# Two weight blocks' low parts moved from VectorE to GpSimd, and a diagonal matrix from VectorE to ScalarE, at the seam between a feed-forward layer and a convolution

## The chip, the cores and the metric

The kernel runs on one core of a Trainium2 chip. The metric is the device time of one execution in microseconds (us). Before the change three runs took 934.97, 930.46 and 936.47 us; their median is 934.97 us. Besides these there is one profiled execution, which took 930.08 us; its trace has a span of 928.3 us.

The engines are named as in the profile: PE is the matrix engine (TensorE) and PEld its weight load, DVE is VectorE, ACT is ScalarE, POOL is GpSimd, SP is SyncE, which issues most of the DMAs.

## The reference

A trunk of two layers over 256 tokens of width 1024, all in fp32. Each layer is a feed-forward block at half weight, a mixer, and a second feed-forward block; the mixer of the first layer is a convolution module, that of the second an attention. The part that matters here is the end of the first feed-forward block of layer 0 and the convolution behind it:

```
h = h + 0.5 * swiglu_ffn(rmsnorm(h, g1), w1, w3, w2)      # (silu(x w1) * (x w3)) w2
m = rmsnorm(h, mix_norm)
u = m @ w_pw1                      # 1024 -> 2048
a, b = split(u);  u = a * sigmoid(b)
u = causal depthwise convolution of width 31 over time
u = silu(rmsnorm(u, g_norm))
h = h + u @ w_pw2                  # 1024 -> 1024, the convolution's last layer
```

## The kernel before

**Split operands.** Most matmuls are done in three passes. A weight block (128 x 2048) is loaded by SP into a `raw` buffer, ACT rounds it to a high part (`hi`, L161), and DVE takes the difference as a low part (`lo`, L162), each in two pieces of 128 x 1024 (`PIECES` is 2). `mm3` (L271 to L275) then multiplies low by high, high by high and high by low. There are four `raw` buffers and four `hi`/`lo` pairs, used in turn: the load of a block waits until the block four places earlier has been read for the last time. Blocks are listed in one fixed order (`blocks`), and SP issues their loads in that order, so that a load which waits holds up those behind it. A block marked "whole" has no high and low part; its `raw` buffer is read by the matmuls.

The list for the convolution begins with two blocks of the last layer (`cw2[0]` and `cw2[1]`, `conv_block[-1]` and `conv_block[-2]`), which are split and lie ready until the convolution's end. Behind them come the eight blocks of the first layer, whole (`cw1[0]` to `cw1[7]`), and the two remaining blocks of the last layer.

**The end of the feed-forward block.** The output of the down projection (`o`, four PSUM tiles: token block 0 or 1 by column half 0 or 1) is partly computed by a scheme that trades matmuls for additions (`fast`); it ends in `fold` (L551 to L559), which adds the partial sums in PSUM (`p`) to the residual `h`: DVE forms L553, L554, L556 and L558, and POOL adds L552, L555, L557 and L559 to `h`. Then `finish` runs the last matmuls tile by tile and adds each tile to `h` on DVE (L566).

**The norm in front of the convolution** (`Plain`). When a column half of `h` is done, ACT squares and sums it (L298). After both halves of token block 0 ACT also loads the table for the sigmoid and runs it once (L422). POOL turns the sum into 1/rms in three small steps (L303, L304, L306; the last is a power). `diagonal` (L427) multiplies the identity by it on DVE, and PE multiplies `h` by this diagonal matrix `dR` (L433), which transposes and normalizes at once; ACT and DVE evict the result by gain (L442, L444). The second half of the matmuls of the last output tile is ordered behind the turn of token block 0, and the turn of token block 1 behind the first product of the convolution.

**The convolution.** PE computes `gate` and `u` (L717) for eight channel blocks; ACT and DVE form `V` (L724, L725). The 31 taps are shared out: DVE has most channel blocks (L759, L761), POOL adds the products that ACT makes for three of them (L775, L779, L780, L781), PE does the rest as matmuls (L790). Then come the second norm (L808 to L840) and the last layer (L901 and `mm3`).

**What sets the order.** The framework simulates the program and orders each engine's instructions by it; a function marked `@urgent` goes ahead of other ready work; `behind` keeps the splits behind the last six urgent instructions of an engine; `order` adds a fixed order between two instructions. Each engine runs its own queue strictly in order.

Of the kernel before, what the change touches and what calls it, by code (L numbers as in the profile page):

```python
# [11 lines left out]
F32 = mybir.dt.float32  # L12
# [3 lines left out]
AF = mybir.ActivationFunctionType  # L16
ALU = mybir.AluOpType
# [24 lines left out]
PIECES = 2  # L42
# [38 lines left out]
def trunk(ctx: ExitStack, tc: tile.TileContext, x, xt, pos, invf, gains, gfin, wdw,  # L81
          f1w13, f1w2, f2w13, f2w2, cw1, cw2, wa, wuq, wukv, wo, out):
    nc = tc.nc
# [12 lines left out]
    def uid(s):  # L96
        n_uid[0] += 1
        return f"{s}_{n_uid[0]}"
# [10 lines left out]
    conv_block = {}  # L109
# [20 lines left out]
    loaded = []  # L130
# [4 lines left out]
    def order(ins, first):  # L135
        tc.add_manual_dep(ins.ins, first.name, mybir.DependencyInfo(
            mybir.DependencyClass.NoSync, mybir.DependencyReason.DATA), reason="order")

    def behind(ins):

        for first in ahead_of.get(ins.ins.engine, [])[-BEHIND:]:
            order(ins, first)

    def load(src, pieces=1):
        if isinstance(src, tuple) and src[0] == "fast":
            return load_fast(src[1])
        if isinstance(src, tuple):
            raw = rawp.tile([P, HB], F32, tag="raw", name=uid("raw"))
            nc.sync.dma_start(raw, src[1])
            return raw  # L150
        n = src.shape[-1]
        raw = rawp.tile([P, HB], F32, tag="raw", name=uid("raw"))
        hi = wp.tile([P, HB], F32R, tag="hi", name=uid("hi"))
        lo = wp.tile([P, HB], F32R, tag="lo", name=uid("lo"))
        if len(loaded) < 7:
            fetch(raw[:, :n], src)
        else:
            nc.sync.dma_start(raw[:, :n], src)
        for i in range(pieces):
            c = slice(i * n // pieces, (i + 1) * n // pieces)  # L160
            behind(nc.scalar.copy(hi[:, c], raw[:, c]))  # L161
            behind(nc.vector.tensor_sub(lo[:, c], raw[:, c], hi[:, c].bitcast(F32)))  # L162
        return hi, lo

    def load_fast(src):

        raw = rawp.tile([P, HB], F32, tag="raw", name=uid("raw"))
        sums = rawp.tile([P, HB], F32, tag="raw", name=uid("sums"))
        nc.sync.dma_start(raw, src)
        v = raw.rearrange("p (b n) -> p b n", n=512)  # L170
        t = sums.rearrange("p (b n) -> p b n", n=512)
        behind(nc.gpsimd.tensor_tensor(t[:, 0:2, :], v[:, 0:4:3, :], v[:, 1:2, :].to_broadcast([P, 2, 512]), op=ALU.add))  # L172
        behind(nc.vector.tensor_add(t[:, 2, :], t[:, 0, :], v[:, 3, :]))
        behind(nc.vector.tensor_add(t[:, 3, :], t[:, 2, :], v[:, 2, :]))
        out = []
        for x, cols in ((raw, ((0, 512), (1024, 2048))), (sums, ((0, 1024), (1024, 2048)))):
            hi = wp.tile([P, HB], F32R, tag="hi", name=uid("hi"))
            lo = wp.tile([P, HB], F32R, tag="lo", name=uid("lo"))
            for c0, c1 in cols:
                behind(nc.scalar.copy(hi[:, c0:c1], x[:, c0:c1]))  # L180
                behind(nc.vector.tensor_sub(lo[:, c0:c1], x[:, c0:c1], hi[:, c0:c1].bitcast(F32)))  # L181
            out.append((hi, lo))
        return out
# [24 lines left out]
    def load_to(last):  # L208
        while len(loaded) < last:
            loaded.append(load(blocks[len(loaded)], PIECES))  # L210
# [23 lines left out]
    def fetch(to, src):  # L234

        dma = nc.sync.dma_start(to, src)
        if first_dma:
            order(dma, first_dma[-1].ins)
        first_dma.append(dma)

    fetch(xk[:, :1], xt[:, :1])
    for k in range(KT):
        c = slice(k % 4 * 512, k % 4 * 512 + 512)
# [5 lines left out]
    ident = const.tile([P, P], F32, name="ident")  # L249
    make_identity(nc, ident)  # L250
    neghalf = const.tile([P, 1], F32, name="neghalf")
# [36 lines left out]
    def rstd(src, n, name, scale_in=1.0):  # L288

        ss = small.tile([P, 2], F32, tag="ss", name=uid("ss"))  # L290
        for i in range(2):
            squares(ss, src, n, i, scale_in)
        return power(ss, n, name)

    def squares(ss, src, n, i, scale_in=1.0):
# [2 lines left out]
        nc.scalar.activation(junk[:, :nh], src[:, i * nh:(i + 1) * nh], AF.Square, scale=scale_in,  # L298
                             accum_out=ss[:, i:i + 1])

    def power(ss, n, name):
        ms = small.tile([P, 2], F32, tag="ms", name=uid("ms"))
        nc.gpsimd.tensor_tensor(ms[:, 0:1], ss[:, 0:1], ss[:, 1:2], op=ALU.add)  # L303
        nc.gpsimd.tensor_scalar(ms[:, 1:2], ms[:, 0:1], 1.0 / n, EPS, op0=ALU.mult, op1=ALU.add)  # L304
        r = small.tile([P, 1], F32, tag="r", name=uid(name))
        nc.gpsimd.tensor_tensor(r, ms[:, 1:2], neghalf, op=ALU.pow)  # L306
        return r

    def transposed(src, q, n, after=(), turned=None):
# [25 lines left out]
    class Norm:  # L335
# [26 lines left out]
        def early(self, i):  # L362

            if i == 1:
                self.part(0, 0)
            elif i == 2:
                self.part(0, 1)
                self.rms(0)
            elif i == 3:
                self.part(1, 0)  # L370
# [35 lines left out]
    class Plain:  # L406
# [17 lines left out]
        @urgent  # L424
        def diagonal(self, tb):
            r = power(self.ss[tb], D, "R")
            nc.vector.tensor_scalar(self.dg[tb], ident, r, None, op0=ALU.mult)  # L427

        @urgent
        def turn(self, tb, q, after=()):  # L430
# [15 lines left out]
        def early(self, i):  # L446
            self.half(i // 2, i % 2)
            if i % 2 == 1:
                self.diagonal(i // 2)
            if i == 2:  # L450

                for q in range(2):
                    self.turn(0, q)
# [822 lines left out]
def build(shapes):  # L1276
    import concourse.bacc as _bacc

    nc = _bacc.Bacc("TRN2", target_bir_lowering=False, num_devices=1, dynamic_dma_scratch_size=1024)
    args = [nc.dram_tensor(f"in_{n}", s, mybir.dt.from_np(np.dtype(d)), kind="ExternalInput").ap()  # L1280
            for n, s, d in shapes]
    out = nc.dram_tensor("out", (S, D), F32, kind="ExternalOutput").ap()
    with tile.TileContext(nc, schedule_with_timeline_sim=True) as tc:
        trunk(tc, *args, out)
    return nc
# [9 lines left out]
```

## Time and profile before

| | |
|---|---|
| Three runs | 934.97, 930.46, 936.47 us (median 934.97) |
| Profiled execution | 930.08 us, of which 928.3 us span |
| PE busy | 913.5 us, 98% of the span |
| DVE busy | 687.6 us, 74% |
| ACT busy | 536.4 us, 58% |
| POOL busy | 213.4 us, 23% |
| Bytes moved | 191.58 MB, 206 GB/s in the mean |

A row of the timeline is: start in us, duration in us (of the whole merged group), engine, line, operation, output <- input, shape, count, and in brackets the idle time of the engine before it and what ended it. [...] A row of the stages gives the stage, its length, the busy time of PE, PEld, DVE, ACT and POOL with the number of instructions, the granted PE clock, the share of the DMA engines and the GB/s.

### The profile page before, as it was taken

The numbers are of one execution on the slowest core, as the hardware profiler recorded it, in microseconds if no ns is written. First come the engines' busy times: TensorE is split into PE (matmuls) and PEld (weight loads), VectorE is DVE, ScalarE is ACT, GpSimd is POOL, SyncE is SP. The second block draws the span as 40 slices with busy tenths as digits, with TensorE's granted clock in tenths as the row PEclk, the third lists the DMA queues.
The fourth block names the chain that finished last, engine by engine and source line by source line (L and its number), as shares of the span: only waits on it lengthen the run. The fifth ranks groups of instructions, "written<-read, shape, count | busy, mean of one in ns | idle before, by whom it ended". The sixth has DMA issues, their size and how long they took to land.

```text
span 928.3 us, 12409 instructions
## 1 busy us (share of the span) xinstructions
PE 913.5 (98%) x4337; PEld 761.0 (82%) x4337; DVE 687.6 (74%) x1047; ACT 536.4 (58%) x928; POOL 213.4 (23%) x325
## 2 busy tenths in 40 slices
PE   9999999899999999999999999999999999999997
PEld 7888888798977888888888888888898778888886
DVE  5777787889974667778876667878666476667975
ACT  6964465558865445455575445655667374544643
POOL 1110222349931001222210003223200010003223
PEclk9999999999999999999999999999999999999999
DMA  9986555823323866565857765657451557774651
GB/s 340 348 291 231 203 170 216 317 90 139 137 91 127 299 243 237 184 196 198 308 198 237 246 233 184 193 206 262 181 182 46 182 204 236 254 246 150 226 181 46
DMA packets 60399, 191.58 MB, mean 206 GB/s; under 512 B 11184, under 2 KB 33328, under 8 KB 40752
## 3 DMA queue, kind: packets, MB, share of 16 engines
q1 hardware_dynamic: 59760, 190.09, 58.7%
q8 instruction: 34, 0.56, 0.2%
q10 hardware_dynamic: 576, 0.69, 0.2%
q14 instruction: 29, 0.24, 0.1%
HBM read 178.17 MB, written 12.58 MB: 205 GB/s over the span
## 4 chain that ended last, share of the span: by engine, by line
PE 89%; DVE 5%; ACT 3%; DMA 1%; issue 1%; SPq 0%; POOLq 0%; ACTq 0%; POOL 0%; DVEq 0%
PE u L275 17%; PE u L271 17%; PE u L274 17%; PE o L271 6%; PE o L274 6%; PE o L275 6%; DVE lo L162 3%; PE u L717 3%; PE gate L717 3%; PE p L275 2%; PE p L271 2%; PE p L274 2%; PE o L901 2%; PE y L790 2%; ACT hi L161 1%
## 5 line engine op out<-in xcount | busy, mean ns | idle before, releaser
L162 DVE TENSOR_TENSOR lo<-raw,hi 128x1024 fp32r<-128x1024 f32 (+1 forms) x250 | 304.9, 1255 | 76.9 <-ACT hi L161 76.8
L161 ACT CAST hi<-raw 128x1024 fp32r<-128x1024 f32 (+1 forms) x250 | 248.0, 1046 | 153.3 <-PE u L275 111.1
L275 PE MATMUL u<-hi,Xl 128*128 128x512 f32 x688 | 267.8, 390 | 0.7 <-DVE Xl L330 0.7
L271 PE MATMUL u<-lo,Xh 128*128 128x512 f32 x688 | 268.1, 390 | 0.1
L274 PE MATMUL u<-hi,Xh 128*128 128x512 f32 x688 | 267.7, 389 | 0.0
L275 PEld LDWEIGHTS u<-hi,Xl 128*128 128x128 f32 x688 | 129.2, 188 | 28.5 <-DVE Xl L330 1.6
L271 PEld LDWEIGHTS u<-lo,Xh 128*128 128x128 f32 x688 | 129.2, 188 | 26.8 <-DVE lo L162 0.5
L274 PEld LDWEIGHTS u<-hi,Xh 128*128 128x128 f32 x688 | 129.2, 188 | 26.8
L271 PE MATMUL o<-lo,Gh 128*128 128x512 f32 (+1 forms) x236 | 91.0, 386 | 0.0
L275 PE MATMUL o<-hi,Gl 128*128 128x512 f32 (+1 forms) x236 | 91.0, 385 | 0.0
L274 PE MATMUL o<-hi,Gh 128*128 128x512 f32 (+1 forms) x236 | 91.0, 385 | 0.0
L172 POOL TENSOR_TENSOR sums<-raw 128x1024 f32<-128x1024 f32 x20 | 53.1, 2653 | 161.2 <-DMA raw<-in_f2w 52.6
L611 POOL TENSOR_TENSOR sx<-gb 128x128 f32<-128x128 f32 x20 | 10.4, 521 | 311.9 <-DMA gb<-gd 311.9
L181 DVE TENSOR_TENSOR lo<-sums,hi 128x1024 fp32r<-128x1024 f32 x40 | 56.1, 1433 | 0.0
L603 ACT CAST Gh<-gb 128x512 fp32r<-128x512 f32 (+2 forms) x48 | 25.6, 539 | 49.8 <-DMA gb<-gd 49.6
L761 DVE SCALAR_TENSOR_TENSOR acc<-V,dw,acc 128x256 f32<-128x256 f32 (+1 forms) x160 | 54.0, 417 | 0.1
L180 ACT CAST hi<-sums 128x1024 fp32r<-128x1024 f32 x40 | 40.7, 1052 | 22.5 <-PE u L275 15.3
L604 DVE TENSOR_TENSOR Gl<-gb,Gh 128x512 fp32r<-128x512 f32 (+2 forms) x48 | 33.1, 704 | 26.4 <-ACT Gh L603 26.4
L275 PEld LDWEIGHTS o<-hi,Gl 128*128 128x128 f32 x236 | 44.3, 188 | 9.0
L274 PEld LDWEIGHTS o<-hi,Gh 128*128 128x128 f32 x236 | 44.3, 188 | 9.0
L271 PEld LDWEIGHTS o<-lo,Gh 128*128 128x128 f32 x236 | 44.3, 188 | 8.7
L180 ACT CAST hi<-raw 128x512 fp32r<-128x512 f32 (+1 forms) x40 | 31.4, 834 | 34.7 <-PE o L275 27.8
(246 smaller groups left out, 1336.6 us busy)
## 6 DMA issues: line engine op xcount, KB each, us to landing
raw<-in_f2w SPq DMA_DIRECT2D x66, 1024.0 KB, 4.8
raw<-in_f1w SPq DMA_DIRECT2D x64, 1024.0 KB, 5.3
raw<-in_cw SPq DMA_DIRECT2D x12, 1024.0 KB, 6.0
gd<-gt SPq DMA_DIRECT2D x160, 64.0 KB, 2.5
gb<-gd SPq DMA_DIRECT2D x40, 256.0 KB, 3.0
raw<-in_wo SPq DMA_DIRECT2D x4, 1024.0 KB, 4.9
raw<-in_wuq SPq DMA_DIRECT2D x3, 1024.0 KB, 4.7
raw<-in_f1w SPq DMA_DIRECT2D x8, 256.0 KB, 6.2
```

Source lines behind the costliest of these rows:

```text
L161: behind(nc.scalar.copy(hi[:, c], raw[:, c]))
L162: behind(nc.vector.tensor_sub(lo[:, c], raw[:, c], hi[:, c].bitcast(F32)))
L172: behind(nc.gpsimd.tensor_tensor(t[:, 0:2, :], v[:, 0:4:3, :], v[:, 1:2, :].to_broadcast([P, 2, 512]), op=ALU.add))
L180: behind(nc.scalar.copy(hi[:, c0:c1], x[:, c0:c1]))
L181: behind(nc.vector.tensor_sub(lo[:, c0:c1], x[:, c0:c1], hi[:, c0:c1].bitcast(F32)))
L271: mm = nc.tensor.matmul(o, ah, bl, start=start, stop=False)
L274: nc.tensor.matmul(o, ah, bh, start=False, stop=False)
L275: return nc.tensor.matmul(o, al, bh, start=False, stop=stop)
L603: nc.scalar.copy(dh, x)
L604: nc.vector.tensor_sub(dl, x, dh.bitcast(F32))
L717: mm = nc.tensor.matmul(u[:, t], w[:, c], X.x[:, k, t], start=(k == 0), stop=(k == KT - 1))
L761: nc.vector.scalar_tensor_tensor(out if j == j1 - 1 else y, v, w, y, op0=ALU.mult, op1=ALU.add)
```

## The change

Two things change, both at this seam.

The low parts of the two split blocks `cw2[0]` and `cw2[1]` are no longer taken by DVE when the blocks are loaded. Their operands are kept in a list (`low_later`), and `lows` takes them by POOL, two pieces (one block) behind the power of each of the norm's two token blocks. The diagonal matrix is made by ACT (a copy of the identity, scaled by the 1/rms of each row) and no longer by DVE.

```diff
+    low_later = []
+
     def load(src, pieces=1):
...
+        later = len(loaded) in (conv_block[-1], conv_block[-2])
...
             behind(nc.scalar.copy(hi[:, c], raw[:, c]))
-            behind(nc.vector.tensor_sub(lo[:, c], raw[:, c], hi[:, c].bitcast(F32)))
+            if later:
+                low_later.append((lo[:, c], raw[:, c], hi[:, c].bitcast(F32)))
+            else:
+                behind(nc.vector.tensor_sub(lo[:, c], raw[:, c], hi[:, c].bitcast(F32)))
...
+    raised = []
+
     def power(ss, n, name):
...
-        nc.gpsimd.tensor_tensor(r, ms[:, 1:2], neghalf, op=ALU.pow)
+        raised.append(nc.gpsimd.tensor_tensor(r, ms[:, 1:2], neghalf, op=ALU.pow))
...
         def diagonal(self, tb):
             r = power(self.ss[tb], D, "R")
-            nc.vector.tensor_scalar(self.dg[tb], ident, r, None, op0=ALU.mult)
+            nc.scalar.activation(self.dg[tb], ident, AF.Copy, scale=r)
+
+        def lows(self, n):
+
+            for _ in range(n):
+                order(nc.gpsimd.tensor_tensor(*low_later.pop(0), op=ALU.subtract), raised[-1].ins)
...
             if i % 2 == 1:
                 self.diagonal(i // 2)
+                self.lows(PIECES)
```

On DVE, from the last splits of the feed-forward block to the turn of token block 0, the queue before was as follows (`lo_1538` and `lo_1546` are the low parts of the two blocks, `h_79` and `h_80` the two token blocks of the residual, `o_1193` to `o_1195` the first three output tiles):

```order
L162 TENSOR_TENSOR lo_1495<-raw_1493,hi_1494 128x1024 x2
L162 TENSOR_TENSOR lo_1538<-raw_1536,hi_1537 128x1024
L553 TENSOR_TENSOR fold_1525<-p_1206,fold_1522 128x512
L162 TENSOR_TENSOR lo_1538<-raw_1536,hi_1537 128x1024
L554 TENSOR_TENSOR fold_1523<-p_1207,fold_1525 128x512
L556 TENSOR_TENSOR fold_1526<-p_1208,fold_1525 128x512
L162 TENSOR_TENSOR lo_1546<-raw_1544,hi_1545 128x1024 x2
L558 TENSOR_TENSOR fold_1524<-p_1208,fold_1523 128x512
L566 TENSOR_TENSOR h_79<-o_1193,h_79 128x512
L566 TENSOR_TENSOR h_79<-o_1194,h_79 128x512
L566 TENSOR_TENSOR h_80<-o_1195,h_80 128x512
L427 TENSOR_SCALAR dR_1568<-ident,R_1592 128x128
```

In the changed kernel (whose line numbers are up to 14 higher; L567 to L572 are the fold, L580 the addition to `h`) the same stretch is:

```order
L168 TENSOR_TENSOR lo_1495<-raw_1493,hi_1494 128x1024 x2
L567 TENSOR_TENSOR fold_1525<-p_1206,fold_1522 128x512
L568 TENSOR_TENSOR fold_1523<-p_1207,fold_1525 128x512
L570 TENSOR_TENSOR fold_1526<-p_1208,fold_1525 128x512
L572 TENSOR_TENSOR fold_1524<-p_1208,fold_1523 128x512
L580 TENSOR_TENSOR h_79<-o_1193,h_79 128x512
L580 TENSOR_TENSOR h_79<-o_1194,h_79 128x512
L580 TENSOR_TENSOR h_80<-o_1195,h_80 128x512
L457 TENSOR_SCALAR Xp_1561<-tp_1608,G 128x128
```

The four subtractions between the fold's steps are gone, and so is the diagonal matrix.

On POOL, behind the fold's last addition, stood the norm of the two token blocks, the clearing of the padding of `V`, and then the taps:

```order
L559 TENSOR_TENSOR h_80<-h_80,fold_1524 128x512
L303 TENSOR_TENSOR ms_1589<-ss_1566 128x1
L304 TENSOR_SCALAR ms_1589<-ms_1589 128x1
L306 TENSOR_TENSOR R_1592<-ms_1589,neghalf 128x1
L705 MEMSET V 128x8x30
L303 TENSOR_TENSOR ms_1643<-ss_1567 128x1
L304 TENSOR_SCALAR ms_1643<-ms_1643 128x1
L306 TENSOR_TENSOR R_1646<-ms_1643,neghalf 128x1
L780 TENSOR_TENSOR Y<-Y,prod_2078 128x128
```

In the changed kernel the two blocks' subtractions (L440) stand behind each power (L314):

```order
L573 TENSOR_TENSOR h_80<-h_80,fold_1524 128x512
L311 TENSOR_TENSOR ms_1585<-ss_1562 128x1
L312 TENSOR_SCALAR ms_1585<-ms_1585 128x1
L314 TENSOR_TENSOR R_1588<-ms_1585,neghalf 128x1
L440 TENSOR_TENSOR lo_1538<-raw_1536,hi_1537 128x1024 x2
L719 MEMSET V 128x8x30
L311 TENSOR_TENSOR ms_1641<-ss_1563 128x1
L312 TENSOR_SCALAR ms_1641<-ms_1641 128x1
L314 TENSOR_TENSOR R_1644<-ms_1641,neghalf 128x1
L440 TENSOR_TENSOR lo_1544<-raw_1542,hi_1543 128x1024 x2
L794 TENSOR_TENSOR Y<-Y,prod_2078 128x128
```

The second token block's norm and the first tap now each have two subtractions of 128 x 1024 in front of them.

On ACT, in the changed kernel, each diagonal matrix (L435) stands behind the squares of its token block (L304), the first one also behind the table load and the sigmoid (L430):

```order
L304 ACTIVATE junk_1566,ss_1562<-h_79 128x512
L304 ACTIVATE junk_1581,ss_1562<-h_79 128x512
L430 ACT_TABLE_LOAD
L430 ACTIVATE sigm<-ss_1562 128x1
L435 ACTIVATE dR_1564<-ident,R_1588 128x128
L304 ACTIVATE junk_1606,ss_1563<-h_80 128x512
```

Before, the third square followed the sigmoid directly; no further table load was added.

## The prediction

> **What bounds the kernel now.** I read the page first: the busy times, and the chain that ended last.
>
> ```profile
> span 928.3 us, 12409 instructions
> PE 913.5 (98%) x4337; PEld 761.0 (82%) x4337; DVE 687.6 (74%) x1047; ACT 536.4 (58%) x928; POOL 213.4 (23%) x325
> PE 89%; DVE 5%; ACT 3%; DMA 1%; issue 1%; SPq 0%; POOLq 0%; ACTq 0%; POOL 0%; DVEq 0%
> ```
>
> PE is the bound, and the chain leaves it for little. So an edit on DVE, ACT and POOL gains only where PE waits, and at most that wait. Next come the stages around the seam.
>
> ```profile
> 168.00:182.50 14.50, 14.48 (x64) 11.64 (x63) 13.15 (x12) 6.65 (x8) 6.44 (x4) 1.00 0.85 310
> 182.50:188.80 6.30, 3.45 (x24) 3.22 (x25) 2.10 (x6) 4.55 (x12) 1.38 (x4) 1.00 0.37 155
> 188.80:246.00 57.20, 57.20 (x336) 52.27 (x335) 54.49 (x163) 44.63 (x124) 46.53 (x95) 1.00 0.37 130
> ```
>
> PE is idle in the middle stage alone (3.45 of 6.30 us busy); ahead of it DVE is nearly full (13.15 of 14.50), behind it PE never rests for 57 us. The timeline of PE shows the wait as one hole:
>
> ```profile
> 178.01 0.39 PE L275 MATMUL o<-hi,Gl 128*128 128x512 f32 x1
> 182.09 0.39 PE L275 MATMUL o<-hi,Gl 128*128 128x512 f32 x1
> 185.35 2.02 PE L433 MATMUL tp<-dR,h 128*128 128x128 f32 x16 [2.87 <-ACT sigm L422]
> 193.74 1.95 PE L433 MATMUL tp<-dR,h 128*128 128x128 f32 x16
> ```
>
> The row names the sigmoid, but what the matmul reads is `dR`. Where that was late, the other engines' timelines tell, DVE's first:
>
> ```profile
> 165.39 2.35 DVE L162 TENSOR_TENSOR lo<-raw,hi 128x1024 fp32r<-128x1024 f32 x2
> 169.33 4.60 DVE L162 TENSOR_TENSOR lo<-raw,hi 128x1024 fp32r<-128x1024 f32 x3 [1.59 <-ACT hi L161]
> 176.78 4.18 DVE L162 TENSOR_TENSOR lo<-raw,hi 128x1024 fp32r<-128x1024 f32 x2
> 180.88 0.68 DVE L558 TENSOR_TENSOR fold<-p,fold 128x512 f32<-128x512 f32 x1
> 181.48 1.87 DVE L566 TENSOR_TENSOR h<-o,h 128x512 f32<-128x512 f32 x3
> 184.96 0.29 DVE L427 TENSOR_SCALAR dR<-ident,R 128x128 f32<-128x128 f32 x1 [1.61 <-POOL R L306]
> ```
>
> The three additions to `h` (L566) begin at 181.48, right behind the last fold. The second of them reads the output tile whose last matmul began at 178.01, so it stood about 3 us behind four pieces of L162 that nobody needs before the convolution's end. ACT and POOL then follow without a pause:
>
> ```profile
> 183.00 0.63 ACT L298 ACTIVATE junk<-h 128x512 f32<-128x512 f32 x1
> 183.54 0.19 ACT L298 ACTIVATION_READ_ACCUMULATOR junk<-h 128x1 f32 x1
> 183.74 1.28 ACT L422 ACT_TABLE_LOAD   x1
> 185.04 0.20 ACT L422 ACTIVATE sigm<-ss 128x1 f32<-128x1 f32 x1
> 184.36 0.57 POOL L306 TENSOR_TENSOR R<-ms,neghalf 128x1 f32<-128x1 f32 x1
> ```
>
> The squares end at 183.73, the power at 184.93, `dR` at 185.25, and PE starts at 185.35. The releaser is DVE's queue.
>
> **The part on DVE: what goes, and what is late next.** L162 loses its last four pieces here. They cost more than their own work:
>
> ```profile
> 170.80 2.04 POOL L552 TENSOR_TENSOR h<-h,fold 128x512 f32<-128x512 f32 x1 [12.93 <-ACT fold L551]
> 176.34 1.30 POOL L555 TENSOR_TENSOR h<-h,fold 128x512 f32<-128x512 f32 x1 [3.50 <-DVE fold L554]
> 177.60 2.28 POOL L557 TENSOR_TENSOR h<-h,fold 128x512 f32<-128x512 f32 x1
> 181.64 1.28 POOL L559 TENSOR_TENSOR h<-h,fold 128x512 f32<-128x512 f32 x1 [1.76 <-DVE fold L558]
> ```
>
> The same POOL addition takes 1.28 us beside L566 and 2.28 us beside L162, and the two L162 at 176.78 take 4.18 us where the two at 165.39 take 2.35: the two engines took turns. [...]
>
> Without the four, the first fold waits for its partial sum on PE:
>
> ```profile
> 171.89 0.39 PE L275 MATMUL p<-hi,Sl 128*128 128x512 f32 x1
> ```
>
> It ends at 172.28, so L553 can start at 172.35; four fold steps 0.6 apart end by 174.9, and POOL's last three additions of 1.3 us follow the second step (173.65): done by 177.6. All that is over before the output tile of 178.01 ends at 178.40. The second L566 then runs from 178.44 to 179.12 (0.68 us), the second square with its read to 179.89 (0.72 us by the rows at 183.00 to 183.73), and `R` is ready 1.20 us later by the old distance (183.73 to 184.93), at 181.1. What is late next is ACT, not POOL: table load and sigmoid end 1.51 us behind the square (183.73 to 185.24), at 181.40.
>
> **The diagonal on ACT.** No row has this copy from SBUF with a scale per row on the identity; the nearest is one with such a scale and size:
>
> ```profile
> 198.72 0.40 ACT L775 ACTIVATE Y<-V,dw 128x128 f32<-128x128 f32 x1 [1.44 <-DVE V L725]
> ```
>
> I take 0.40 us (from below the 0.29 of DVE's L427, from above 0.63, the 512-wide square): `dR` ends at 181.8, PE may start 0.1 later, at 181.9. PE's own queue reaches the turn at 182.09 + 0.23 = 182.32. So the hole closes with 0.4 us to spare, and the start moves from 185.35 to 182.32: **a gain of 3.0 us**. Were the copy 0.63 us, the spare would still be 0.2. Queued behind ACT's wait for `R` is the third square, which needs the third L566 at about 181.9, and only token block 1 waits for it.
>
> **The part on POOL.** Four subtractions of 128 x 1024 are new there. POOL has one operation of that size:
>
> ```profile
> L172 POOL TENSOR_TENSOR sums<-raw x20: 2392/2401/3874, 98.6 to 892.5; 128x1024 f32<-128x1024 f32 x20
> 188.83 0.30 POOL L705 MEMSET V<- 128x240 f32 x1 [3.90 <-PE o L275]
> 190.33 0.19 POOL L303 TENSOR_TENSOR ms<-ss 128x1 f32<-128x1 f32 x1 [1.20 <-ACT junk L298]
> 199.79 0.46 POOL L780 TENSOR_TENSOR Y<-Y,prod 128x128 f32<-128x128 f32 x1 [8.35 <-ACT prod L779]
> ```
>
> I take 2.40 us each, the median of 20 (bounds 2.39 and 3.87; rounding to fp32r on writing stands in no POOL row). The first two run from 181.1 to 185.9, the padding (0.3 us) to 186.2. The second norm's sum comes 3 us earlier than at 190.33, at 187.3: POOL is free, with 1.1 us over. `R` of token block 1 is ready 1.1 us later (1.20 from the square, as above), at 188.4, `dR` at 188.8, and PE asks for it at 193.74 - 3.0 = 190.7. The next two subtractions run to 193.2; the first tap, 3 us earlier than 199.79, comes at 196.8. At 3.87 us each the norm would end at 190.3 (`dR` 190.8, PE 0.2 late) and the subtractions at 198.0, with the taps 1.2 us behind the shift. What of that reaches PE stands at the end of the convolution:
>
> ```profile
> 261.39 0.44 POOL L781 TENSOR_TENSOR part<-part,odd 128x128 f32<-128x128 f32 x1
> 262.92 0.29 DVE L876 TENSOR_TENSOR Y<-y,part 128x128 f32<-128x128 f32 x1 [0.99 <-PE y L790]
> ```
>
> The taps end at 261.83 and are needed at 262.92, so they have 1.1 us. The upper price therefore costs 0.3 us together, a gain of 2.7.
>
> [...]
>
> The two `raw` buffers are now released later, and SP's queue waits in order:
>
> ```profile
> 175.69 0.33 SPq L149 DMA_DIRECT2D raw<-in_cw  x1
> 180.99 0.33 SPq L149 DMA_DIRECT2D raw<-in_cw  x1
> raw<-in_cw SPq DMA_DIRECT2D x12, 1024.0 KB, 6.0
> 204.68 3.62 PE L717 MATMUL gate<-Xp,raw 128*128 128x256 f32 x16
> 211.59 3.62 PE L717 MATMUL gate<-Xp,raw 128*128 128x256 f32 x16
> ```
>
> These two loads waited for DVE and now wait for POOL: issued at 186 and 193.3 in place of 175.69 and 180.99, landing 6.0 us later by the median, at 192 and 199.3. PE reads them at 204.68 and 211.59, less 3.0: 201.7 and 208.6. Both are covered by 9 us; if POOL were later by that much, PE would wait for the difference.
>
> **The sum.** -3.0 us on PE; 0 for POOL, DMAs and ACT, each covered as said. Behind the seam PE, DVE and POOL are all nearly full up to the second norm, and all their first inputs come from PE, so the streams move as one. The later layers are PE's too (98% busy), and their loads are set off by PE's progress. The profiled execution becomes 930.08 - 3.0 = 927.1 us. It lies 4.9 below the median of the three runs shown; 934.97 - 3.0 gives **932.0 us**, -0.3%. A difference within about 1% is what a measurement of this kernel can hardly tell from none, the runs themselves lying 0.6% apart.
>
> **The rivals.**
>
> *Later streams eat the gain (the taps do not move with PE).* DVE has 54.49 of 57.20 us busy behind the seam, POOL 46.53, nearly all of it behind its first tap. If POOL's new work slowed DVE's taps as it slowed L162, or itself finished late, the convolution would end by the taps. Against it speak two rows of DVE's taps:
>
> ```profile
> 193.96 2.15 DVE L761 SCALAR_TENSOR_TENSOR acc<-V,dw,acc 128x128 f32<-128x128 f32 x8
> 205.34 6.30 DVE L761 SCALAR_TENSOR_TENSOR acc<-V,dw,acc 128x128 f32<-128x128 f32 x24
> ```
>
> The first eight ran with POOL idle, the later 24 beside POOL's taps, and both follow each other 0.26 us apart (`acc` lies in PSUM, so they have one input in SBUF). The price is the shift less POOL's room: gain 1.0, 929.1 profiled and 934.0 as the median.
>
> *The change does not do what it says: the hole stays, under another name.* If the second L566 or the squares were held elsewhere (their scratch buffers are freed by POOL's additions, which I put at 177.6), or ACT's copy waited longer, every microsecond over the 0.4 of spare is lost again; with 3.4 the gain is gone: 930.1, median 935.0. For it: the profile's releaser is ACT's sigmoid, and `dR` now stands behind it on purpose. Against it: in the new sum the sigmoid ends at 181.4, 0.9 us before PE is free.
>
> *Slower: GpSimd's subtraction is much dearer than its addition.* This form, with the rounding to fp32r, has no row. With x us a piece, POOL's first pair delays the second norm, and the second pair the taps: once 2x is over 5.9 us, `R` comes at 182.5 + 2x and the taps at 182.5 + 4x. Before, they began at 199.79 and had 1.1 us of room; the balance lies at 182.5 + 4x = 200.9, x = 4.6 us. From there each further microsecond a piece costs four. At twice the dearest POOL row (7.75) the taps begin at 213.5: 12.6 us slower, 942.7 profiled, 947.6 as the median. Against it: the dearest row is 3.87, and that in turns with DVE.
>
> **How the numbers follow.** The forecast (2.5 to 3.2 us gained) gets 0.70, the taps that eat the gain 0.14, the hole under another name 0.09, the dear subtraction 0.07. The range: the three runs less 3.0 span 927.5 to 933.5; the copy's and the subtraction's bounds add 0.3, the profiled execution less 3.0 widens the lower end to 927, and I go to 926.5; the two rivals without gain reach to 936.5 (the highest run). The dear subtraction is left out with a little scatter. Faster by over 1% needs a gain of 9 us, which no case has; only scatter of the runs gives it 0.05. Slower by over 1% is the dear subtraction with x over 6.9 and scatter: 0.06. The rest, 0.89, is within 1%.
>
> **What would show it.** Right: PE without a hole before the first L433 and that row at about 182.3; L566 in three rows, apart, at about 175.8, 178.4 and 181.2; L552 still near 2 us, L557 at 1.3; four POOL subtractions near 2.4 us; the first POOL tap near 196.8; the two loads landing before 202; the rows from the first turn to the second norm all 3 us earlier. Wrong: a POOL subtraction over 4.6 us, L761 longer than 0.35 us between 188 and 194, or a new idle time of PE at L433 or L717.

## The result and the profile after

The changed kernel takes 927.87 us (median of 8 runs, 927.38 to 929.89) against 934.91 us for the kernel before (8 runs beside it, 930.46 to 936.47). The ratio is 0.9935 with a 95% interval of 0.9918 to 0.9953: 6.1 us faster, between 4.4 and 7.7. (The ratio compares all runs of both kernels and is not the quotient of the medians, which lie 7.0 us apart.) The prediction had the sign, and its range (926.5 to 936.5) holds the time, near its lower end; its gain of 3.0 us is half of what was measured. The profiled execution took 928.00 us, only 2.1 us less than the profiled one of before. So there are two questions: did the mechanism work as foretold, and where are the other 3 us?

The page after, span and busy times:

```profile
span 926.2 us, 12414 instructions
PE 913.4 (99%) x4337; PEld 761.0 (82%) x4337; DVE 680.1 (73%) x1041; ACT 537.6 (58%) x930; POOL 222.0 (24%) x329
```

DVE has 7.5 us less work and POOL 8.6 us more; PE has the same, in a shorter span. The stages around the seam after the change (from 168 us to the last matmul ahead of the turn, to the first product, to the second norm):

```profile
168.00:182.87 14.87, 14.87 (x67) 12.30 (x66) 7.74 (x10) 9.86 (x15) 7.66 (x8) 1.00 0.65 262
182.87:186.28 3.41, 3.41 (x25) 3.10 (x24) 0.83 (x3) 1.84 (x6) 3.41 (x2) 1.00 0.00 0
186.28:260.70 74.42, 74.20 (x485) 69.05 (x483) 68.76 (x212) 57.54 (x158) 67.25 (x134) 1.00 0.40 142
```

PE is busy throughout. Its timeline at the place of the hole:

```profile
182.87 0.40 PE L281 MATMUL o<-hi,Gl 128*128 128x512 f32 x1
183.11 1.95 PE L446 MATMUL tp<-dR,h 128*128 128x128 f32 x16
186.28 0.38 PE L731 MATMUL gate<-Xp,raw 128*128 128x128 f32 x2
```

From the last matmul ahead of the turn to the turn it is 0.24 us (183.11 - 182.87), where before it was 3.26 (185.35 - 182.09): 3.02 us are gone here. The prediction adds 0.23 us to 182.09, which is how far apart matmuls that follow each other start in the profile of before; each shows 0.39 us, so that the rows overlap. The two ahead of 182.09:

```profile
181.64 0.39 PE L271 MATMUL o<-lo,Gh 128*128 128x512 f32 x1
181.87 0.39 PE L274 MATMUL o<-hi,Gh 128*128 128x512 f32 x1
```

This execution reached the place 0.78 us later than the one of before (182.87 against 182.09, with nothing changed up to there), and from the first product to the end it takes 0.2 us more (739.9 us against 739.7); that leaves the 2.1 us between the two profiles. The later arrival begins at the start of the kernel, where a weight block landed later (ACT, waiting for the DMA, begins to cast it at 12.23 us, before at 11.43); PE's wait for it, before and after:

```profile
12.51 0.73 PE L280 MATMUL u<-hi,Xh 128*128 128x512 f32 x2 [0.47 <-ACT Xh L391]
13.31 0.73 PE L286 MATMUL u<-hi,Xh 128*128 128x512 f32 x2 [1.39 <-ACT Xh L399]
```

The timelines of DVE, ACT and POOL after the change, one fence each:

```profile
175.10 0.68 DVE L572 TENSOR_TENSOR fold<-p,fold 128x512 f32<-128x512 f32 x1
177.86 0.69 DVE L580 TENSOR_TENSOR h<-o,h 128x512 f32<-128x512 f32 x1 [2.08 <-PE o L281]
179.29 0.69 DVE L580 TENSOR_TENSOR h<-o,h 128x512 f32<-128x512 f32 x1 [0.74 <-PE o L281]
```

```profile
180.63 0.19 ACT L304 ACTIVATION_READ_ACCUMULATOR junk<-h 128x1 f32 x1
182.13 0.20 ACT L430 ACTIVATE sigm<-ss 128x1 f32<-128x1 f32 x1
182.24 0.39 ACT L435 ACTIVATE dR<-ident,R 128x128 f32<-128x128 f32 x1
```

```profile
175.92 1.29 POOL L571 TENSOR_TENSOR h<-h,fold 128x512 f32<-128x512 f32 x1
181.99 4.72 POOL L440 TENSOR_TENSOR lo<-raw,hi 128x1024 fp32r<-128x1024 f32 x2
188.07 0.19 POOL L311 TENSOR_TENSOR ms<-ss 128x1 f32<-128x1 f32 x1 [1.11 <-ACT junk L304]
189.15 4.67 POOL L440 TENSOR_TENSOR lo<-raw,hi 128x1024 fp32r<-128x1024 f32 x2
197.20 0.46 POOL L794 TENSOR_TENSOR Y<-Y,prod 128x128 f32<-128x128 f32 x1 [3.38 <-ACT prod L793]
```

The second addition to `h` now waits for PE's tile and no longer for DVE's queue. `dR` is ready at 182.63, 0.48 us ahead of PE. The subtractions cost 2.36 us each, POOL still waits for the second norm's sum (1.11 us idle) and for the first tap (3.38 us). The items foretold for this execution are there, but for the first addition to `h`: it was put at about 175.8 and comes at 177.86, of which 0.78 are the later arrival. It waits for PE's tile, and the second one, which counts, comes where it was foretold. The missing 3 us are not in this execution.

### The profile page after: what moved, and what is told of

The parts are those of the page before. It is cut to its first block, busy times and chain, and to the rows that moved or that the text cites. A ratio compares the mean times of both kernels' runs of the same rounds, so it can differ in the third digit from the quotient of the medians.

```text
span 926.2 us, 12414 instructions
## 1 busy us (share of the span) xinstructions
PE 913.4 (99%) x4337; PEld 761.0 (82%) x4337; DVE 680.1 (73%) x1041; ACT 537.6 (58%) x930; POOL 222.0 (24%) x329
## 4 chain that ended last, share of the span: by engine, by line
PE 89%; ACT 3%; DVE 3%; issue 1%; DMA 1%; POOL 1%; POOLq 0%; SPq 0%; ACTq 0%
PE u L281 17%; PE u L277 17%; PE u L280 17%; PE o L277 6%; PE o L280 6%; PE o L281 6%; PE gate L731 3%; PE u L731 3%; DVE lo L168 2%; PE p L277 2%; PE p L280 2%; PE p L281 2%; PE o L915 2%; ACT hi L164 1%; DMA raw<-in_f1w 1%
## 5 line engine op out<-in xcount | busy, mean ns | idle before, releaser
L168 DVE TENSOR_TENSOR lo<-raw,hi 128x1024 fp32r<-128x1024 f32 (+1 forms) x246 | 297.8, 1247 | 74.4 <-ACT hi L164 74.1
```

## The experiments

The ratio is always to the kernel before, run on the same chip in turns; of that kernel 30 executions each stand beside the first four and beside the last four.

**The kernel before, once more.** No edit. 

> The kernel before, run as a kernel of its own, to see its scatter beside its granted clock and span. The prediction's theory (the hole of 2.9 us in front of the first L433 costs its own length and nothing else): ratio 1.000 to the kernel before, the hole in its profile again 2.8 to 3.0 us; the rest of the measured gain over 3.0 us then lies in executions that are slower for another reason, somewhere else. Rival (the hole costs more than its length in most executions, because PE runs at a lower granted clock behind it, or because DVE's queue is longer in them): a profile of an execution that takes 934 us or more shows a lower clock behind the hole, or a hole of 5 to 7 us.

Measured: 934.41 us (931.00 to 936.21, 12 runs), ratio 1.000 (0.9986 to 1.0015). Its profile fell on an execution of 933.95 us, 3.9 us more than the one the prediction was made from, and shows what that one did not. PE at the seam, and the stages cut 3.4 us long:

```profile
182.50 0.39 PE L275 MATMUL o<-hi,Gl 128*128 128x512 f32 x1
186.77 3.75 PE L433 MATMUL tp<-dR,h 128*128 128x128 f32 x16 [3.88 <-ACT sigm L422]
192.45 0.38 PE L717 MATMUL gate<-Xp,raw 128*128 128x128 f32 x2
```

```profile
182.50:184.90 2.40, 0.39 (x2) 0.00 (x0) 2.27 (x4) 1.21 (x3) 1.27 (x1) 1.00 0.54 164
184.90:188.30 3.40, 1.53 (x7) 1.56 (x8) 0.28 (x1) 2.34 (x6) 0.96 (x3) 0.53 0.46 193
188.30:191.70 3.40, 3.40 (x15) 3.11 (x15) 1.05 (x3) 1.44 (x4) 0.00 (x0) 0.50 0.00 0
191.70:195.10 3.40, 3.40 (x28) 3.26 (x27) 0.95 (x2) 0.74 (x3) 1.06 (x4) 0.97 0.00 0
```

Two things differ. The granted clock falls to 0.50 inside the hole, at about 185.1 and so 2.2 us after PE's last matmul had ended, and stays there for two of these stretches; the 16 matmuls of the turn take 3.75 us in place of 2.02. And the hole is 3.88 us long in place of 2.87. From the last matmul ahead of the turn to the first product it is 9.95 us (192.45 - 182.50); in the first profile it was 6.51 (188.60 - 182.09), after the change it is 3.41. Of the 3.44 us more than in the first profile, 1.01 are the longer hole and 2.43 the slower clock. Against this execution the change gains 6.5 us at this place. The first product in the first profile:

```profile
188.60 0.38 PE L717 MATMUL gate<-Xp,raw 128*128 128x128 f32 x2
```

Why the hole was longer, ACT's timelines of the first profile and of this execution show:

```profile
168.24 2.01 ACT L161 CAST hi<-raw 128x1024 fp32r<-128x1024 f32 x2 [3.39 <-PE o L275]
169.66 2.00 ACT L161 CAST hi<-raw 128x1024 fp32r<-128x1024 f32 x2 [4.35 <-DMA raw<-in_f1w]
```

The cast waited for PE in the first profile and waits here for a load, a block of the feed-forward layer. It begins 1.42 us later, and DVE's additions to `h` also begin 1.42 us later (182.90 against 181.48), while PE reaches the turn only 0.41 us later (182.50 against 182.09): the difference is the 1.01 us. How often that happens, one profile can't tell.

The mean granted clock that each execution reports says how often the clock falls. Of 72 executions of the kernel before (30 + 30 beside the others, and these 12):

| mean granted clock | executions | time, us |
|---|---|---|
| 0.998 | 12 | 930.37 to 931.30 |
| 0.997 or less | 60 | 931.43 to 936.60 |

The prediction was made from an execution (clock 0.998) of the rarer kind.

**The hole filled with useless work.** The kernel before, with small matmuls on zeros ahead of the last output tile, so that PE arrives at the turn later and does not rest there.

```diff
...
+                        if i == 2 and isinstance(nxt, Plain):
+                            keep_warm(24, "B", end)
                         nxt.early(i)
```

`end` is the last matmul of the third output tile.

> The kernel before with 24 small matmuls on zeros (about 2.6 us) in front of the last output tile's matmuls, so that PE's queue reaches the turn 2.6 us later and hardly rests there; the diagonal is as late as before. Nothing of the result is changed. Plain hole: the same time as before (934.9, ratio 1.000). If an idle PE costs more than the idle time itself: 930 to 932, ratio 0.995 to 0.997.

Measured: 930.92 us (930.30 to 932.76, 11 runs), ratio 0.9973 (0.9958 to 0.9988). Nothing arrives earlier, PE does 2.6 us more work, and the kernel is 2.5 us faster (1.1 to 3.9). No execution reports a clock below 0.998. The added work and PE's wait in the profile:

```profile
181.27 2.79 PE L263 MATMUL warm<-still 128*128 128x256 bf16 x24
185.61 2.05 PE L433 MATMUL tp<-dR,h 128*128 128x128 f32 x16 [0.16 <-DVE dR L427]
```

That rules out the plain hole: a resting PE cost more than the time it rested. DVE's queue is that of the kernel before, so the diagonal is as late as there, and the 2.5 us are the clock's part of the gain and not that of a longer hole, as far as the added work changes nothing else. With the clock kept, the kernel before stands at 930.9. The changed kernel, in other comparisons, lies at 927.9, which is 3.0 us below; by the ratios it is 2.5 to 3.6 us. The gain that was foretold, 3.0, is in that.

**The hole put back by another engine.** The changed kernel, with the first diagonal matrix made seven times on ACT.

```diff
-            nc.scalar.activation(self.dg[tb], ident, AF.Copy, scale=r)
+            for _ in range(1 + 6 * (tb == 0)):
+                nc.scalar.activation(self.dg[tb], ident, AF.Copy, scale=r)
```

> The changed kernel with the hole put back by another engine: ACT makes the first diagonal matrix seven times over in place of once (each must wait for the one before), so that it is ready some 3.4 us later. DVE, POOL and the DMAs stay as in the changed kernel. Hole about 3 us by its profile. Plain hole: 928 + 3 = 931, ratio to the kernel before 0.996. If an idle PE costs more than its length: 934 to 935, ratio 0.999 to 1.000. If the gain beyond 3 us came from DVE's or POOL's other work: 931 as well, so that it is e4 that tells those two apart.

Measured: 931.70 us (930.51 to 933.95, 12 runs), ratio 0.9982 (0.9966 to 0.9997), between the two expectations. The copies followed each other faster than I had reckoned (the last five took 2.12 us together, and I had put some 3.4 us for the six added), and the hole is 2.50 us, not 3. PE's timeline, and then the stages behind the hole:

```profile
187.33 3.06 PE L447 MATMUL tp<-dR,h 128*128 128x128 f32 x16 [2.50 <-ACT dR L436]
```

```profile
187.30:188.10 0.80, 0.77 (x6) 0.77 (x7) 0.00 (x0) 0.00 (x0) 0.80 (x1) 1.00 0.00 0
188.10:191.50 3.40, 3.40 (x16) 3.11 (x15) 1.02 (x3) 1.38 (x4) 0.14 (x1) 0.51 0.62 212
191.50:195.00 3.50, 3.50 (x29) 3.36 (x28) 1.96 (x5) 0.80 (x3) 1.11 (x4) 0.99 0.23 94
```

Here the clock falls after the hole, when PE had been at work again for 0.8 us, and for one stretch of 3.4 us. Of the 12 executions six report 0.998 (930.51 to 932.00 us) and six 0.997 or less (931.05 to 933.95). A plain hole of 2.5 us would put the changed kernel at 930.4. The executions without a drop lie close to that or up to 1.6 above it, and a lower clock is reported by half of the 12, without any of DVE's or POOL's work being different.

**The low parts alone.** The changed kernel with `dR` made by DVE as before.

```diff
-            nc.scalar.activation(self.dg[tb], ident, AF.Copy, scale=r)
+            nc.vector.tensor_scalar(self.dg[tb], ident, r, None, op0=ALU.mult)
```

> Half of the change alone: the low parts by POOL, the diagonal matrix still by DVE. If the hole closes by DVE's queue alone, the diagonal on DVE is ready 0.3 us behind R and PE has no hole: the same time as the changed kernel (928). If DVE's copy of the identity has to wait for POOL's first subtraction, which starts in the same moment, it comes 2.4 us late, and PE has a hole of about 1.6 us: 929.5 to 930; if it waits for both, 4.7 us and a hole of about 4: 932.

Measured: 930.04 us (928.40 to 931.70, 8 runs), ratio 0.9955 (0.9939 to 0.9971). The second case holds, as the timelines of DVE, POOL and PE show:

```profile
183.80 2.38 DVE L435 TENSOR_SCALAR dR<-ident,R 128x128 f32<-128x128 f32 x1 [2.08 <-POOL R L314]
```

```profile
183.73 4.69 POOL L440 TENSOR_TENSOR lo<-raw,hi 128x1024 fp32r<-128x1024 f32 x2
```

```profile
186.28 2.02 PE L446 MATMUL tp<-dR,h 128*128 128x128 f32 x16 [1.28 <-issue]
```

A copy that took 0.29 us takes 2.38 beside POOL's first subtraction, which began 0.07 us earlier; PE waits 1.28 us. None of the 8 executions reports a clock below 0.998. So the second half of the change, ACT for the diagonal, is what keeps the first half from making a new, shorter hole.

**The diagonal alone.** The kernel before with the same line of `diagonal` changed the other way (ACT for DVE). 

> The other half alone: the diagonal matrix by ACT, the low parts still by DVE. DVE's queue stays as it was, so the squares are as late as before, and on ACT the diagonal now comes behind the sigmoid and the third square: ready 0.7 to 1.1 us later than by DVE. Hole 3.6 to 4.0 us where the kernel before has 2.9. Plain hole: 0.7 to 1.1 us slower than before (ratio 1.001). With the clock halved behind nearly every hole of that length: 1 to 2.5 us slower (ratio 1.001 to 1.003).

Measured: 934.63 us (933.34 to 936.89, 12 runs), ratio 1.0016 (0.9999 to 1.0033), 1.5 us slower by the middle, not told apart from none, so that the time decides between neither expectation. The hole in the profile is 3.71 us, and all 12 executions report 0.997 or less. PE's timeline:

```profile
187.02 3.59 PE L433 MATMUL tp<-dR,h 128*128 128x128 f32 x16 [3.71 <-ACT dR L427]
```

**The low parts by DVE, but later.** All four subtractions on DVE, behind its second addition to `h`; the diagonal on ACT.

```diff
-                order(nc.gpsimd.tensor_tensor(*low_later.pop(0), op=ALU.subtract), raised[-1].ins)
+                behind(nc.vector.tensor_sub(*low_later.pop(0)))
...
             if i % 2 == 1:
                 self.diagonal(i // 2)
-                self.lows(PIECES)
+                if i == 1:
+                    self.lows(2 * PIECES)
```

> As the changed kernel, but the four subtractions are done by DVE behind its second addition to h, in the idle time of DVE between that and the eviction of the turn, and not by POOL. If what counts is that they leave the place in front of the additions: no hole, 927.5 to 928.5, the same as the changed kernel (ratio to before 0.993 to 0.995). If it counts that DVE has less work: DVE's taps, nearly full behind the seam, end up to 2 us later: 929 to 930.

Measured: 928.60 us (927.79 to 930.63, 12 runs), ratio 0.9954 (0.9939 to 0.9969). It lies between the two cases and not apart from the changed kernel beside it (0.9946). What is left of a hole is not due to DVE's taps but to POOL's small steps of the norm (timeline rows of POOL and, last, of PE):

```profile
182.79 1.05 POOL L312 TENSOR_SCALAR ms<-ms 128x1 f32<-128x1 f32 x1
183.92 1.43 POOL L314 TENSOR_TENSOR R<-ms,neghalf 128x1 f32<-128x1 f32 x1
185.84 2.05 PE L446 MATMUL tp<-dR,h 128*128 128x128 f32 x16 [1.04 <-ACT dR L435]
```

The first two took 0.19 and 0.57 us in the changed kernel; here they run beside DVE's four subtractions, which fill DVE from 181.44 to 186.06 us. So most of the gain comes from taking the four pieces out of the way of the additions; who does them later matters for about a microsecond in the profile.

**Twice the work on POOL.** Each of POOL's four subtractions done twice.

```diff
+                args = low_later.pop(0)
+                for _ in range(2):
+                    order(nc.gpsimd.tensor_tensor(*args, op=ALU.subtract), raised[-1].ins)
```

> The changed kernel with each of POOL's four subtractions done twice, so that a block costs 9.4 us in place of 4.7. By the prediction's account of POOL (norm of token block 1 late once a block takes over 5.9 us, taps with 1.1 us of room): the second turn waits about 1.7 us on PE, the first tap comes about 4.5 us later than in the changed kernel, and the end of the convolution 3.4 us: 931 to 931.5 (ratio to before 0.996 to 0.997). If POOL's taps have more room than that: 929.5 to 930. If a late first tap costs in full: 932 to 933.

Measured: 932.22 us (930.87 to 933.22, 12 runs), ratio 0.9983 (0.9967 to 0.9999): 4.3 us more than the changed kernel's 927.95 beside it, where 3.0 to 3.6 were expected. Three rows of its profile, PE's waits:

```profile
195.53 0.49 PE L733 MATMUL gate<-Xp,raw 128*128 128x128 f32 x2 [1.45 <-ACT Xp L457]
262.26 0.49 PE L846 MATMUL rb<-dg,ones 128*128 128x128 f32 x2 [1.35 <-DVE dg L844]
263.56 2.98 PE L917 MATMUL o<-raw,Z 128*128 128x512 f32 x4 [0.81 <-ACT Z L853]
```

POOL's lateness appears where the prediction's account puts it: once behind the norm of token block 1 (1.45 us, 1.7 expected), once at the end of the taps. The row at 263.56 takes 2.98 us where it takes 1.98 to 1.99 elsewhere: two short waits close together were followed by a drop of the clock, too, as the stage behind them shows:

```profile
265.00:266.00 1.00, 1.00 (x2) 0.34 (x1) 0.58 (x2) 1.00 (x4) 0.00 (x0) 0.50 0.00 0
```

**The changed kernel once more.** No edit. 

> The changed kernel once more, on the same chip as these three and with as many runs. Both theories: ratio to the kernel before 0.993 to 0.995, runs within 2.5 us of each other, where those of the kernel before spread over 6 us, since there is no hole behind which the clock can drop. A profile with a lower granted clock between 183 and 193 us, or a hole there, would speak against it.

Measured: 927.95 us (926.94 to 929.15, 7 runs), ratio 0.9946 (0.9925 to 0.9968). Its profile has no wait of PE at the turn, as the two rows show, and a clock of 1.00 in every microsecond from 181 to 196.

```profile
184.02 0.40 PE L281 MATMUL o<-hi,Gl 128*128 128x512 f32 x1
184.25 1.95 PE L446 MATMUL tp<-dR,h 128*128 128x128 f32 x16
```

Beside it six executions of the kernel before reported a clock of 0.998; they took 930.63 to 931.13 us (median 930.72), and the changed kernel is 2.8 us below them. So on one chip, too, the hole alone is worth about the 3.0 us foretold.

The 15 executions of the changed kernel in the two comparisons lie between 926.94 and 929.89. Three of them report 0.997, at 927.50, 927.74 and 928.70 us, and so without a visible cost; a mean over the whole execution does not say where the clock was low.

**All profiles side by side.** From the first product of the convolution to the end, every profile takes 739.7 to 740.0 us, except that of the doubled work (744.4). So the kernels differ at the seam, and by when an execution arrives there. From the last matmul ahead of the turn to the first product it is, in us:

| kernel | profiled execution | at the seam |
|---|---|---|
| before, first profile | 930.08 | 6.51 |
| before, once more | 933.95 | 9.95 |
| diagonal alone | 933.59 | 8.91 |
| hole put back | 933.95 | 7.78 |
| low parts alone | 931.33 | 4.92 |
| low parts by DVE, later | 930.55 | 4.71 |
| hole filled | 930.41 | 3.84 |
| changed | 928.00 | 3.41 |
| changed, once more | 929.15 | 3.40 |

The last matmul ahead of the turn starts between 182.09 and 184.61 us in these profiles (at 182.5 with the hole filled, less the 2.6 us of added work). That scatter is nearly as large as the hole, and nothing ahead of that place was changed on PE.

## Why the prediction was right in sign and half in size

**What bounds the seam: right.** PE waited for `dR`, `dR` for the squares, these for L566, and L566 for four pieces of L162 ahead of it in DVE's queue: its second addition began at 182.08, though its tile's last matmul ended at 178.40. Taking the pieces away moved the turn by 3.02 us in the profile, against 3.0.

**The turns of DVE and POOL: right.** L571 (L557 before) takes 1.29 us in place of 2.28. Two runs show the same from the other side: `dR` on DVE 2.38 us beside a subtraction on POOL, and POOL's steps of the norm 1.05 and 1.43 us beside subtractions on DVE. `dR` on DVE took 0.29 us in the first profile of before; it has one tensor input and a scale per row. Which operations of the two engines hold each other up was not shown beyond these pairs, nor that the one input in SBUF, which the prediction remarks on for L761, has a part in it.

**The diagonal on ACT: right.** 0.39 us against 0.40; spare 0.48 against 0.4. That ACT had to be the engine was not seen: on DVE the copy meets POOL's subtraction (2.38 us in place of 0.29).

**The price on POOL and its cover: right.** 2.36 us a piece against 2.40; idle time ahead of the second norm 1.11 against 1.1. With the work doubled, the delays came as the account says, and the total of 4.3 us was 0.7 to 1.3 above it, with a drop of the clock that the account does not have. The slower rival, with its balance at 4.6 us a piece, was not near at 2.36. Doubled, at 4.7 us a piece, the kernel took 932.22, about 1.5 us above the executions of before without a drop and 1.9 below the median of all of them, so the balance is placed to within a microsecond or two at best.

**The loads: right.** The two issues moved to the end of POOL's subtractions:

```profile
186.74 0.33 SPq L151 DMA_DIRECT2D raw<-in_cw  x1
193.84 0.33 SPq L151 DMA_DIRECT2D raw<-in_cw  x1
```

They were put at 186 and 193.3, the place being reached 0.8 us later in this execution; PE did not wait for either.

**The streams behind the seam: right.** The first tap comes at 197.20 (196.8 foretold, plus the 0.8), and the rival of later streams did not come: the last layer's first matmul, after and before, starts 2.08 us earlier, 2.9 if the 0.8 is counted.

```profile
262.02 1.98 PE L915 MATMUL o<-raw,Z 128*128 128x512 f32 x4 [0.81 <-ACT Z L851]
264.10 1.99 PE L901 MATMUL o<-raw,Z 128*128 128x512 f32 x4 [1.06 <-ACT Z L837]
```

**The step that failed** is the first one: an edit there "gains only where PE waits, and at most that wait", and with it the term "a gain of 3.0 us". The wait cost more than itself. Behind it the granted clock was 0.50 in the profile of an execution of 933.95 us, for some 6.8 us, which cost 2.43 us, and the hole itself was 1.01 us longer there. With the hole filled by useless work the kernel before gains 2.5 us (1.1 to 3.9), and the changed kernel lies about 3 us below that. The term should have read: 3.0 for the hole, and about 3 for what follows it in most executions. The same step shows in the two times that the prediction gave: 927.1 for the profiled execution was within 1 us of what the changed kernel takes (928.00 in its profile, 927.87 in the median), while 932.0, which took the 3.0 from the median of slower executions, was 4.1 too high. That the range holds the measured time is owed to its lower end, which was widened to the profiled execution less 3.0; the cost that the sum lacks is in no part of it.

A sign of it stood in front of me. The runs of before lay 0.4 to 6.4 us above the profiled execution; I took that for scatter, and most of it was the cost of the same hole. The one profile that the prediction went by showed a clock of 1.00 behind its hole of 2.87 us. The length of a hole alone does not tell when the clock falls: it fell after a hole of 2.50 us, and in the hole of 3.88 us it fell when PE had rested for 2.2. By what rule it falls was not shown.

**What stays open.** How often the hole is longer than 2.87 us, and so how the gain beyond the clock's 2.5 us is made up: only one profile of a slower execution of the kernel before was taken, and a load's landing decided its hole. Where the 0.3% between single executions of the changed kernel come from is seen in part: its two profiles reach the seam 1.15 us apart (182.87 and 184.02), and their times differ by the same 1.15. Why loads land at different times was not looked for.

## What to carry to other kernels

A short rest of the matrix engine, where it is the bound, can cost 1.6 times its length by the clock that is granted behind it (3.88 us of rest and 2.43 of slower clock in one profile); so closing such a hole can gain more than the hole is long, and even filling it with useless work can gain (2.5 us here). When the runs of a kernel lie above its profiled execution, first look whether the profiled one is of the cheaper kind: the mean clock of each run is the first hint (here 0.998 against 0.997 or less). And before work is moved between DVE and POOL, look at what the two will do in the same moment: here a copy of 0.29 us became one of 2.38.

## What the runs showed of the hardware that I had not expected

A hole on PE of 2.50, of 3.71 and of 3.88 us was followed by a granted clock of 0.50 (one profile each), one of 2.87 us was not. Nor does it take one long hole: waits of 1.35 and 0.81 us close together were followed by it, too. Over all executions, those reporting a clock of 0.997 or less were 0 of 31 where the profiled hole was 0.16, 1.04 and 1.28 us, 6 of 12 at 2.50 us, 60 of 72 for the kernel before (2.87 and 3.88 us) and 12 of 12 at 3.71 us. The count is no clean sign: 3 of the 15 executions of the changed kernel, whose two profiles have no hole there, are among those as well, and 7 of the 12 with POOL's work doubled. The low clock lasted 3.4 us or twice that, cost 1.6 to 2.4 us (from the turn to the first product 4.81, 4.89 and 5.68 us, against 3.25 and 3.17 without a drop), and could begin 0.8 us after the hole had ended, on matmuls that were running back to back.
